# The order of the first three MLP blocks, the split of the first loads, the warming and a late sum in a two-layer decoder trunk

## The chip, the cores and the metric

One core of a Trainium2 chip runs the whole program. The metric is the device time of one execution in microseconds (us). The engines are TensorE (PE, matmuls), VectorE (DVE), ScalarE (ACT), GpSimd (POOL) and SyncE (SP, which issues DMAs); ACT and POOL issue DMAs too.

## The reference

The program computes two layers of a decoder trunk in float32, with 512 tokens of width 1024. Layer 0 has a latent attention mixer (MLA), layer 1 a gated linear attention mixer (GLA). Behind each mixer stands an MLP with a squared ReLU and 4096 hidden columns, and at the end a norm:

```python
def sq_relu_mlp(xn, w_up, w_down):
    hid = jnp.square(jax.nn.relu(xn @ w_up))
    return hid @ w_down

for i in range(DEPTH):
    x = x + mixer_i(rms_norm(x, norm_mix[i]))
    x = x + sq_relu_mlp(rms_norm(x, norm_mlp[i]), w_up[i], w_down[i])
return rms_norm(x, final_norm)
```

## The kernel before

**Numbers in two parts.** A float32 operand is split into a high and a low part that PE takes. ACT writes the high part of weights (`wh`, L112), DVE the low part (`wl`, L115). A product is three matmuls a tile: high by high, high weight by low data, low weight by high data. `wh` and `wl` have three buffers each.

**The start.** `load_x` (L168) loads x in eight parts of 256 KB, `load_part` (L1559) the first weights (`wraw_ckv`, 1 MB) in three, k-tiles 0 to 2, 2 to 4 and 4 to 8; ACT's queue takes x parts 0 and 2 and the gains (L1563), SP's the rest. `wraw` of the next product follows on SP. While they come, ten matmuls on ones (L1576, two records each in the profile) keep PE busy. For each weight part ACT and DVE split it (L112, L115), then scale and split the x parts with it (`scaled`, L245 on ACT and L246 on DVE, tiles `set`). The first phase of PE is 48 matmuls of 512 columns on the eight `set` pairs (L120 to L122); then the next product begins, whose weights are `wraw`, cut by `piece` in L451 and after.

**The MLP.** Up and down projections are each done in blocks by a scheme of seven products in place of eight. A product is 24 matmuls of 256 columns (L825): 16 with `wh` and 8 with `wl` (the latter in pairs on one weight tile). Eight blocks b make the hidden columns. `up_block(b)` gives a list of steps: s1 makes product 11, s2 21, s5 T1, s6 T2, s3 22, s7 T3, s4 T4 (s0 prepares). Bank x1 of PSUM holds 11 and then 21; x5 holds T1 and then 22; the bank `seed` (there is one, `b2`) starts as a copy of 11 (L925 on ACT) and takes T2, T3 and T4 one after the other, adding to what it holds. Between them it is read: after T2 by ACT (L951, `u2`), after T3 by DVE (L963, `q`, with the copy `p5` of T1), after T4 by `finish` (L889 on DVE, then a square on ACT, L890). DVE also makes sums of weight quarters: L948 and L954 for T2 and 22. The tiles `mt` (four buffers) hold `p1`, `p5` and `u2`; weight quarters lie in `raw` (five buffers) and come over SP (L864) or, adding to what is there, over POOL (L878).

`down_block(s)` gives the steps of the down projection, which stand between those of later up blocks. At the end of an MLP, L1043 to L1045 add the last products to the residual; L1045, `acc[4] += acc[6]`, is the late sum.

**What sets the order.** The program is written as straight code. Each engine runs its instructions in the order in which a scheduler lays them out from the order of the code, and waits on semaphores. Around the change the list returned by `up_block` and the loop over blocks in the MLP decide. In the loop, all steps of block 0 come first, then all of block 1 and so on; a down step is put behind every second one.

## Time and profile before

| | us |
|---|---|
| three runs | 1067.56, 1068.91 (median), 1069.22 |
| the profiled execution | 1068.29 |
| its span | 1066.6 |
| PE busy | 1048.6 (98%) |
| DVE busy | 856.7 (80%) |
| ACT busy | 640.1 (60%) |

The profiled execution's own time is 1.7 above its span, which runs from the first to the last recorded instruction. All times within the trace count from the start of the span. A row of a timeline has the start, the length, the engine, the line, the operation with output and inputs, the shape, a count where equal neighbours are joined, and in brackets how long the engine had been idle and what ended that. Busy time of PE contains overlaps of pipelined matmuls, so their pace is read from starts.

### The profile page before, as it was taken

How to read it: one execution, taken by the hardware profiler on the slowest of the kernel's cores; microseconds unless marked ns; L12 is line 12 of the kernel's file. 1: busy time of each engine (PE TensorE's matmuls, PEld its weight loads, DVE VectorE, ACT ScalarE, POOL GpSimd, SP SyncE). 2: the span in 40 equal slices, each digit the busy share in tenths (PEclk: the TensorE clock that was granted, in tenths of full speed). 3: DMA queues.
4: the chain of work that ended last, by engine and by line, in shares of the span. 5: the costliest groups of instructions: out<-in, count | busy, mean ns of one | idle time of the engine just before them, and what ended most of it. 6: DMA issues, size and time to landing. Idle time of an engine off the chain costs nothing.

```text
span 1066.6 us, 17924 instructions
## 1 busy us (share of the span) xinstructions
PE 1048.6 (98%) x7322; PEld 967.8 (91%) x7322; DVE 856.7 (80%) x1185; ACT 640.1 (60%) x934; POOL 77.9 (7%) x104
## 2 busy tenths in 40 slices
PE   8999999999999999999999999999999999999997
PEld 6788888989999999998788888888999999999986
DVE  6789879899899789966565654668999799799865
ACT  6577645665666776654334734655666667775734
POOL 6400000000000000030000000001000000000000
PEclk9999999999999999999999999999999999999999
DMA  6412016865554663351122212238564555653412
GB/s 204 105 50 79 1 40 196 180 179 137 166 139 132 178 147 117 94 193 43 50 80 80 80 48 71 80 98 216 163 137 139 169 129 158 187 128 103 139 39 80
DMA packets 113874, 126.76 MB, mean 119 GB/s; under 512 B 8592, under 2 KB 85664, under 8 KB 113792
## 3 DMA queue, kind: packets, MB, share of 16 engines
q1 hardware_dynamic: 98048, 107.62, 31.7%
q0 software_dynamic: 13792, 16.80, 10.1%
q10 hardware_dynamic: 1952, 1.21, 0.4%
q8 instruction: 57, 0.93, 0.4%
q14 instruction: 25, 0.20, 0.1%
HBM read 123.51 MB, written 2.10 MB: 118 GB/s over the span
## 4 chain that ended last, share of the span: by engine, by line
PE 93%; DVE 5%; DMA 1%; issue 1%; ACT 0%; SPq 0%; DVEq 0%
PE ps L825 46%; PE ps L120 13%; PE ps L122 13%; PE ps L121 13%; PE ps L137 2%; DVE wl L115 2%; PE ps L1406 2%; DMA wraw_ckv<-in_mla_w_in_dram 1%; PE ps L1445 0%; PE ps L684 0%; DVE raw L948 0%; PE ps L685 0%; PE ps L683 0%; PE ps L682 0%; PE ps L681 0%
## 5 line engine op out<-in xcount | busy, mean ns | idle before, releaser
L112 ACT ACTIVATE wh<-raw 128x1024 fp32r<-128x1024 f32 x208 | 219.7, 1059 | 139.6 <-PE ps L825 86.1
L115 DVE TENSOR_TENSOR wl<-raw,wh 128x1024 fp32r<-128x1024 f32 x208 | 251.5, 1220 | 22.6 <-ACT wh L112 22.0
L825 PE MATMUL ps<-h,wh 128*128 128x256 f32 x1344 | 166.6, 276 | 0.0
L825 PEld LDWEIGHTS ps<-h,wh 128*128 128x128 f32 x1344 | 159.2, 188 | 0.0
L120 PE MATMUL ps<-set,wh 128*128 128x512 f32 x232 | 91.6, 395 | 1.7 <-ACT set L245 1.7
L121 PE MATMUL ps<-set,wh 128*128 128x512 f32 x232 | 91.5, 394 | 1.0 <-DVE set L246 0.9
L825 PE MATMUL ps<-h,wl 128*128 128x256 f32 x672 | 90.4, 277 | 1.8 <-DVE wl L115 1.8
L122 PE MATMUL ps<-set,wl 128*128 128x512 f32 x232 | 91.3, 394 | 0.0
L112 ACT ACTIVATE wh<-wraw 128x1024 fp32r<-128x1024 f32 x41 | 43.0, 1057 | 73.7 <-PE ps L122 41.5
L825 PEld LDWEIGHTS ps<-h,wl 128*128 128x128 f32 x672 | 82.7, 188 | 2.2 <-DVE wl L115 2.2
L878 POOL DMA_DIRECT2D raw<-in_mlp_w_up_dram x20 | 25.8, 1290 | 701.2 <-DVE raw L931 309.0
L890 ACT ACTIVATE q<-q 128x512 f32<-128x512 f32 x64 | 40.3, 630 | 52.9 <-DVE q L889 52.6
L115 DVE TENSOR_TENSOR h<-q,h 128x1024 fp32r<-128x1024 f32 x44 | 53.7, 1222 | 8.3 <-ACT h L112 8.3
L120 PE MATMUL ps<-wh,set 128*128 128x512 f32 x144 | 59.6, 414 | 0.0
L115 DVE TENSOR_TENSOR wl<-wraw,wh 128x1024 fp32r<-128x1024 f32 x41 | 50.3, 1229 | 10.6 <-ACT wh L112 10.5
L122 PE MATMUL ps<-wh,set 128*128 128x512 f32 x144 | 56.3, 391 | 0.0
L121 PE MATMUL ps<-wl,set 128*128 128x512 f32 x144 | 56.2, 390 | 0.0
L121 PEld LDWEIGHTS ps<-set,wh 128*128 128x128 f32 x232 | 44.1, 190 | 11.0 <-DVE set L246 1.9
L120 PEld LDWEIGHTS ps<-set,wh 128*128 128x128 f32 x232 | 43.8, 189 | 10.9 <-ACT set L245 1.9
L122 PEld LDWEIGHTS ps<-set,wl 128*128 128x128 f32 x232 | 44.0, 190 | 9.1
L112 ACT ACTIVATE h<-q 128x1024 fp32r<-128x1024 f32 x44 | 46.0, 1049 | 0.8 <-DVE q L1024 0.8
L825 PE MATMUL ps<-T0h,wh 128*128 128x256 f32 x128 | 32.7, 280 | 5.0 <-DVE q L963 5.0
(512 smaller groups left out, 2779.0 us busy)
## 6 DMA issues: line engine op xcount, KB each, us to landing
raw<-in_mlp_w_down_dram SPq DMA_DIRECT2D x38, 1024.0 KB, 5.2
raw<-in_mlp_w_up_dram SPq DMA_DIRECT2D x68, 512.0 KB, 5.7
wraw<-in_gla_w_in_dram SPq DMA_DIRECT2D x11, 1024.0 KB, 5.2
raw<-in_mlp_w_up_dram POOLq DMA_DIRECT2D x20, 512.0 KB, 6.4
raw<-in_mlp_w_down_dram POOLq DMA_DIRECT2D x6, 1024.0 KB, 9.0
wraw<-in_mla_w_o_dram SPq DMA_DIRECT2D x8, 512.0 KB, 4.9
wraw<-in_gla_w_o_dram SPq DMA_DIRECT2D x8, 512.0 KB, 4.7
xT<-in_x_dram SPq DMA_DIRECT2D x6, 256.0 KB, 7.9
```

Of the source, the lines that this page charges most:

```text
L112: raised.append(order(ACT.activation(hi, src, AF.Copy)))
L115: return lo_eng.tensor_tensor(lo, src, f(hi), ALU.subtract)
L120: PE.matmul(psum, wh, xh, start=start, stop=False, **kw)
L121: PE.matmul(psum, wh, xl, start=False, stop=False, **kw)
L122: PE.matmul(psum, wl, xh, start=False, stop=stop, **kw)
L137: PE.transpose(psum, src, ident[: src.shape[0], : src.shape[0]])
L825: return PE.matmul(p[:, m * TH : (m + 1) * TH], w[i][:, k - k0, m * P : (m + 1) * P], x[k][j], start=start, stop=stop, skip_group_check=True,)
L878: POOL.dma_start(t, rows(half, trail), accum_op=ALU.add)
L890: ACT.activation(qs, qs, AF.Square)
L1406: PE.matmul(p[:, t * 64 : (t + 1) * 64].rearrange("p (n c) -> p n c", c=m), k[:, sl], later, start=True, stop=True)
```

## The change

**The start.** The first weights come in four parts of two k-tiles. ACT's queue issues the gains first, then x parts 0, 2, 3 and 4; SP's the weight parts and x parts 1, 5, 6 and 7. The warming has 15 matmuls. The split of the second product's weights is put behind the last `set` by `issue_after`.

**The blocks.** `up_block` returns other lists for blocks 0 to 2, block 2 also keeps a copy `p1` of its first product, and the read of bank `x5` (`third`) and the doubled sum (`twice`) move with them. The loop takes the steps of blocks 0, 1 and 2 in turn by a row of numbers. The products then follow as T1, T2, 22, T3 of block 0, T1 of block 1, T4 of block 0, 22 and T2 of block 1, 11 of block 2, T3 of block 1, 21 of block 2, T4 of block 1, T1 of block 2. Between any two on one `seed` bank, from T3 of block 0 to the end of block 1, another product stands.

**The late sum** leaves the callback and comes after the last third product.

```diff
--- before.py
+++ after.py
@@ -243,7 +243,7 @@
             hi, lo = slot(self.tag), slot(self.tag)
             g = gcol(self.g, self.g0 + j)
             self.copies[j] = order(ACT.activation(hi, src, AF.Copy, scale=g))
-            DVE.scalar_tensor_tensor(lo, src, g, f(hi), ALU.mult, ALU.subtract)
+            self.low = DVE.scalar_tensor_tensor(lo, src, g, f(hi), ALU.mult, ALU.subtract)
             self.out[j] = (hi, lo)
 
         def add(self, j, src):
@@ -451,7 +451,8 @@
 
         raw = col_chunk(w_in, 0, 256)
         for j in range(2):
-            w = piece(raw[:, :, j * P : (j + 1) * P], ND, P)
+            with tc.issue_after(nrm.copies[-1].ins), tc.issue_after(nrm.low.ins):
+                w = piece(raw[:, :, j * P : (j + 1) * P], ND, P)
             p = bank("c")
             a_type(p, w, X)
             if j == 0:
@@ -914,7 +915,7 @@
                 v["a21"], v["a22"] = unit(1, 0), unit(1, 1)
                 v["x1"] = bank("u")
                 product(v["x1"], a, "11", True)
-                if b == 1:
+                if b in (1, 2):
                     v["p1"] = mt()
                     ACT.activation(v["p1"], v["x1"], AF.Copy)
                 else:
@@ -942,17 +943,29 @@
                 product(v["x1"], v["a12"], "21", False)
                 finish(pairs(v["x1"]), 0, first)
 
+            def twice():
+                DVE.tensor_tensor(v["s"], v["s"], v["a11"], ALU.add)
+
             def s6():
-                if b == 1:
+                if b in (1, 2):
                     seed(v["p1"])
-                DVE.tensor_tensor(v["s"], v["s"], v["a11"], ALU.add)
+                if b != 1:
+                    twice()
                 product(v["b2"], v["s"], "T2", False)
                 v["u2"] = mt()
                 ACT.activation(v["u2"], v["b2"], AF.Copy)
+                if b == 1:
+                    third()
 
             def s3():
+                if b == 1:
+                    twice()
                 DVE.tensor_tensor(v["a12"], v["a12"], v["s"], ALU.add)
                 product(v["x5"], v["a12"], "22", False)
+                if b != 1:
+                    third()
+
+            def third():
                 c = q[1][:, 0:2]
                 DVE.tensor_tensor(c, pairs(v["x5"]), pairs(v["u2"]), ALU.add)
                 finish(c, 0, second)
@@ -967,7 +980,9 @@
                 product(v["b2"], v["a22"], "T4", False)
                 finish(pairs(v["b2"]), 1, first)
 
-            return [s0, s1, s2, s5, s6, s3, s7, s4] if b < 2 else [s1, s5, s2, s6, s3, s7, s4]
+            if b == 1:
+                return [s0, s1, s2, s5, s3, s6, s7, s4]
+            return [s0, s1, s2, s5, s6, s3, s7, s4] if b == 0 else [s1, s2, s5, s6, s3, s7, s4] if b == 2 else [s1, s5, s2, s6, s3, s7, s4]
 
         def down_block(s):
             last = s == NB // 2 - 2
@@ -1042,7 +1057,6 @@
                 def u3(p4):
                     DVE.tensor_tensor(acc[5], p4, acc[5], ALU.add)
                     DVE.tensor_tensor(acc[6], p4, acc[6], ALU.add)
-                    DVE.tensor_tensor(acc[4], acc[4], acc[6], ALU.add)
 
                 product(7, v["21"], b12, u3 if last else None)
 
@@ -1053,6 +1067,8 @@
             def p3():
                 DVE.tensor_tensor(v["S"], v["12"], v["S"], ALU.add)
                 product(3, v["S"], b22)
+                if last:
+                    DVE.tensor_tensor(acc[4], acc[4], acc[6], ALU.add)
 
             def p4():
                 a = quarter(1, 1)
@@ -1163,10 +1179,14 @@
         for b in range(2):
             blocks[b].pop(0)()
         downs = []
-        for b in range(NB):
-            for i, step in enumerate(blocks[b]):
+        for b in (0, 0, 0, 0, 1, 0, 1, 1, 2, 1, 2, 1):
+            blocks[b].pop(0)()
+        assert not blocks[0] and not blocks[1]
+        downs = down_block(0)
+        for b in range(2, NB):
+            for i, step in enumerate(blocks[b], 7 - len(blocks[b])):
                 step()
-                if downs and (i % 2 or (b % 2 and i == 6)):
+                if downs and (i in (2, 3, 5) if b == 2 else i % 2 or (b % 2 and i == 6)):
                     downs.pop(0)()
             if b % 2 and b < NB - 1:
                 downs += down_block(b // 2)
@@ -1558,24 +1578,27 @@
     def load_part(k0, k1):
         SP.dma_start(raw0[:, k0:k1], src0[:, k0:k1])
 
+    ACT.dma_start(gains, t_in["gains"])
+    load_part(0, 2)
     load_x(ACT, 0)
-    load_part(0, 2)
-    ACT.dma_start(gains, t_in["gains"])
     load_x(SP, 1)
     load_x(ACT, 2)
     load_part(2, 4)
-    load_x(SP, 3)
-    load_part(4, 8)
-    for j in range(4, ND):
-        load_x(SP, j)
+    load_x(ACT, 3)
+    load_part(4, 6)
+    load_x(ACT, 4)
+    load_x(SP, 5)
+    load_part(6, 8)
+    load_x(SP, 6)
+    load_x(SP, 7)
     POOL.dma_start(pos_i, t_in["positions"])
     POOL.dma_start(invf, t_in["inv_freq"].to_broadcast([P, 32]))
     exp_set()
     warm = bank("c")
-    for _ in range(10):
+    for _ in range(15):
         PE.matmul(warm[:, :P], ones128, ones128, start=True, stop=True)
     w0 = []
-    for k0, k1 in ((0, 2), (2, 4), (4, 8)):
+    for k0, k1 in ((0, 2), (2, 4), (4, 6), (6, 8)):
         w = piece(raw0[:, k0:k1], k1 - k0, KL, tc.keep_in_program_order)
         w0 += [(w, i) for i in range(k1 - k0)]
         for j in range(k0, k1):
```

PE where T3 of block 0 ends and what follows it, before. `ps_2289` is the `seed` bank of block 0, `T0h` to `T3h` are parts of the data, `wl_2495` the low weights of T3 and `wh_2525` the high weights of T4.

```order
1060 L825 MATMUL ps_2289<-T0h_1953,wl_2495 128x256 x2
1061 L825 MATMUL ps_2289<-T1h_2041,wl_2495 128x256 x2
1062 L825 MATMUL ps_2289<-T2h_2129,wl_2495 128x256 x2
1063 L825 MATMUL ps_2289<-T3h_2332,wl_2495 128x256 x2
1064 L825 MATMUL ps_2289<-T0h_1953,wh_2525 128x256
1065 L825 MATMUL ps_2289<-T0l_1954,wh_2525 128x256
```

The same place after the change, where the bank is `ps_2299` and `ps_2535` is bank `x5` of block 1.

```order
1060 L826 MATMUL ps_2299<-T0h_1963,wl_2505 128x256 x2
1061 L826 MATMUL ps_2299<-T1h_2051,wl_2505 128x256 x2
1062 L826 MATMUL ps_2299<-T2h_2139,wl_2505 128x256 x2
1063 L826 MATMUL ps_2299<-T3h_2342,wl_2505 128x256 x2
1064 L826 MATMUL ps_2535<-T0h_1963,wh_2536 128x256
1065 L826 MATMUL ps_2535<-T0l_1964,wh_2536 128x256
```

T4 of block 0, which came right behind T3, has moved 20 rows on; T1 of block 1 stands there.

DVE around the read of that bank after T3, before the change (L963; L957 is the read of bank `x5`).

```order
389 L957 TENSOR_TENSOR q_2263<-ps_2400,mt_2460 128x512
390 L115 TENSOR_TENSOR wl_2557<-raw_2251,wh_2556 128x1024
391 L889 SCALAR_TENSOR_TENSOR q_2263<-q_2263,rstd_2337 128x512
392 L948 TENSOR_TENSOR raw_2251<-raw_2251,raw_2157 128x1024
393 L963 TENSOR_TENSOR q_2263<-ps_2289,mt_2429 128x512
394 L954 TENSOR_TENSOR raw_2159<-raw_2159,raw_2251 128x1024
395 L889 SCALAR_TENSOR_TENSOR q_2263<-q_2263,rstd_2337 128x512
396 L115 TENSOR_TENSOR wl_2590<-raw_2251,wh_2589 128x1024
397 L889 SCALAR_TENSOR_TENSOR q_2262<-ps_2289,rstd_2337 128x512
```

And after it, where L976 is the read after T3, L970 that of `x5`, L947 and L963 the two sums, and L890 `finish`.

```order
390 L947 TENSOR_TENSOR raw_2261<-raw_2261,raw_2167 128x1024
391 L963 TENSOR_TENSOR raw_2169<-raw_2169,raw_2261 128x1024
392 L970 TENSOR_TENSOR q_2273<-ps_2410,mt_2470 128x512
393 L115 TENSOR_TENSOR wl_2567<-raw_2259,wh_2566 128x1024
394 L890 SCALAR_TENSOR_TENSOR q_2273<-q_2273,rstd_2347 128x512
395 L976 TENSOR_TENSOR q_2273<-ps_2299,mt_2439 128x512
396 L115 TENSOR_TENSOR wl_2599<-raw_2169,wh_2598 128x1024
397 L890 SCALAR_TENSOR_TENSOR q_2273<-q_2273,rstd_2347 128x512
398 L115 TENSOR_TENSOR wl_2629<-raw_2261,wh_2628 128x1024
399 L890 SCALAR_TENSOR_TENSOR q_2272<-ps_2299,rstd_2347 128x512
```

The two sums have moved from around the read to the place ahead of L970; behind the read comes a split (`wl_2599`) at once, and the finish of T4 (the last row) has one more split ahead of it.

DVE at the end of the first MLP, before: L1045 is the late sum, `wl_5163` the low weights that PE's next product takes.

```order
577 L1043 TENSOR_TENSOR xT<-ps_5033,xT 128x4x256
578 L1044 TENSOR_TENSOR sum_0_2244<-ps_5033,sum_0_2244 128x1024
579 L889 SCALAR_TENSOR_TENSOR q_4954<-ps_4962,rstd_2337 128x512
580 L1045 TENSOR_TENSOR xT<-xT,sum_0_2244 128x4x256
581 L115 TENSOR_TENSOR wl_5163<-raw_5155,wh_5162 128x1024
582 L115 TENSOR_TENSOR wl_5191<-raw_5155,wh_5190 128x1024
583 L115 TENSOR_TENSOR wl_5221<-raw_4994,wh_5220 128x1024
584 L115 TENSOR_TENSOR h_5283<-q_4042,h_5283 128x1024
```

And after: the late sum is L1071.

```order
578 L1058 TENSOR_TENSOR xT<-ps_5047,xT 128x4x256
579 L1059 TENSOR_TENSOR sum_0_2254<-ps_5047,sum_0_2254 128x1024
580 L890 SCALAR_TENSOR_TENSOR q_4968<-ps_4976,rstd_2347 128x512
581 L115 TENSOR_TENSOR wl_5176<-raw_5168,wh_5175 128x1024
582 L115 TENSOR_TENSOR wl_5204<-raw_5168,wh_5203 128x1024
583 L115 TENSOR_TENSOR wl_5234<-raw_5008,wh_5233 128x1024
584 L115 TENSOR_TENSOR h_5296<-q_4056,h_5296 128x1024
585 L1071 TENSOR_TENSOR xT<-xT,sum_0_2254 128x4x256
```

The late sum has moved behind three weight splits and a split of `h`.

## Prediction

> **What bounds the kernel now.** I read the page first: its span, its table of engines, and then who TensorE (PE) waits for.
>
> ```profile
> span 1066.6 us, 17924 instructions
> ...
> PE 1048.6 (98%) x7322; PEld 967.8 (91%) x7322; DVE 856.7 (80%) x1185; ACT 640.1 (60%) x934; POOL 77.9 (7%) x104
> ```
> ```profile
> PE ps L825 <- DVE q L963: 5.0, 4, 1.5
> PE ps L825 <- DVE wl L115: 1.8, 2, 1.0
> PE ps L120 <- ACT set L245: 1.7, 1, 1.7
> PE ps L121 <- DVE set L246: 0.9, 1, 0.9
> ```
>
> PE is busy for 1048.6 of 1066.6 us, and the change takes no matmul out of a product. It can only gain where PE idles. The list (total us, times, longest) names 5.0 us in four waits on L963, 1.8 in two waits on a weight split, and 2.6 in two waits at the start. Those three places are the three parts of the change. Next the timeline of PE around the first of the four waits, and at the second (start, duration, instruction, idle time before it).
>
> ```profile
> 214.23 0.40 PE L825 MATMUL ps<-T0h,wl 128*128 128x256 f32 x2
> ...
> 214.94 0.40 PE L825 MATMUL ps<-T3h,wl 128*128 128x256 f32 x2
> 216.84 0.39 PE L825 MATMUL ps<-T0h,wh 128*128 128x256 f32 x1 [1.50 <-DVE q L963]
> ...
> 218.78 0.39 PE L825 MATMUL ps<-T0h,wl 128*128 128x256 f32 x2
> ...
> 219.46 0.39 PE L825 MATMUL ps<-T3h,wl 128*128 128x256 f32 x2
> 231.73 0.39 PE L825 MATMUL ps<-T0h,wh 128*128 128x256 f32 x1 [1.00 <-DVE q L963]
> ```
>
> Two things are to be seen. A wait costs more than its idle figure: two matmuls start from 214.94, so without a wait the next would start at about 215.18; it starts at 216.84, 1.66 late, and a first matmul of 0.39 for 0.28 adds 0.11. The idle 1.50 so stands for 1.77 lost, some 0.27 more. And the pace differs on both sides: six matmuls take 214.94 - 214.23 = 0.71 us before the wait (118 ns each), and 219.46 - 218.78 = 0.68 after it (113 ns). PE has a slow and a quick pace here, and the wait seems to switch it.
>
> **Part 1, the blocks.** The bank that T2, T3 and T4 share must be read by L963 before T4 may add to it. DVE and ACT around that read, and around the next one:
>
> ```profile
> 214.96 1.22 DVE L948 TENSOR_TENSOR raw<-raw,raw 128x1024 f32<-128x1024 f32 x1
> 216.10 0.68 DVE L963 TENSOR_TENSOR q<-ps,mt 128x512 f32<-128x512 f32 x1
> ...
> 219.89 0.69 DVE L889 SCALAR_TENSOR_TENSOR q<-ps,rstd 128x512 f32<-128x512 f32 x1 [0.24 <-PE ps L825]
> ```
> ```profile
> 221.15 0.58 ACT L925 ACTIVATE ps<-mt 128x512 f32<-128x512 f32 x1
> ```
>
> T3 ends at about 215.2 and L963 is read out at 216.78. The change puts a whole product (T1 of block 1) between T3 and T4. A product is 24 matmuls, 24 x 0.1133 = 2.72 us at the quick pace. T4 then starts at about 218.0, and the read has 1.2 us to spare if DVE reaches it when it does today. DVE does: two adds (L948 and L954, 1.22 each) move ahead of the evacuation of block 0's second half, into an idle stretch, and after that a split and a finish stand before the read, as today. So all four waits should go: 5.0 + 4 x 0.27 = 6.1 us gross.
>
> What is late next? Block 1's T2 needs the bank again, seeded from a copy of its first product. Today T4 ends near 219.7, DVE's finish runs 219.89 to 220.58, ACT squares, and the seed ends at 221.73: 2.0 us after T4's end. In the new order one product of 2.72 us lies between (22 of block 1), so 0.7 us is spare. That is the tightest place; a split of 1.22 us ahead of the finish on DVE would use it up. Block 1's own T3 and T4 have a product between them as well, with the same spare 1.2 us, and a third block shares the scheme. Nothing is added on PE; two copies to SBUF replace seeds of the same form (0.58). The order also loads one weight quarter of block 2 a second time, which holds up two later loads; their first use is far enough off that I take it as nothing, and at most the delay of one 512 KB load, some 1.3 us at the rate shown below, if that cover is gone.
>
> Against that stands the pace. If a wait switches PE from 118 to 113 ns, then without it the slow pace goes on. For how long, the trace shows at one kind of place only:
>
> ```profile
> 240.01 2.03 PE L825 MATMUL ps<-h,wh 128*128 128x256 f32 x16
> ...
> 439.11 1.98 PE L825 MATMUL ps<-h,wh 128*128 128x256 f32 x16
> ```
>
> The first down product takes 2.03 for 16 matmuls where a later one takes 1.98: it turns PE slow, (2.03 - 0.28)/15 = 117 ns against 113, and yet the later ones are quick again with no wait listed between 231.73 and the end of the MLP. So the slow pace can end by itself, and I take it that it does so after that down product. Up to it, nine products run in the new order from the old wait on (T1 of block 1, T4 of block 0, 22 and T2 of block 1, 11 of block 2, T3 of block 1, 21 of block 2, T4 of block 1, T1 of block 2): 9 x 24 x 0.0050 = 1.1 us per layer, about 2.0 for two layers with what the restart of today's quick pace costs taken off. Bounds: nothing, if the pace recovers at once; 3.1, half the gross gain, if it lasts somewhat longer. Part 1: -6.1 + 2.0 = -4.1 (-3.0 to -6.1).
>
> **Part 2, the late sum.** The end of the first MLP, DVE and then PE, and PE's same place in the second:
>
> ```profile
> 439.65 1.22 DVE L1045 TENSOR_TENSOR xT<-xT,sum 128x1024 f32<-128x1024 f32 x1
> 440.79 3.49 DVE L115 TENSOR_TENSOR wl<-raw,wh 128x1024 fp32r<-128x1024 f32 x3
> ```
> ```profile
> 442.06 1.19 PE L825 MATMUL ps<-h,wl 128*128 128x256 f32 x8 [0.97 <-DVE wl L115]
> ...
> 989.21 1.20 PE L825 MATMUL ps<-h,wl 128*128 128x256 f32 x8 [0.80 <-DVE wl L115]
> ```
>
> The sum of 1.22 stands right before the split that PE waits for. Moved behind three splits and one split of `h`, it lets the first split start at 439.65 and end at about 440.87; PE wants it after 16 matmuls from 439.11, at 439.11 + 16 x 0.1133 = 440.92. The wait goes, all but 0 to 0.1. Gain: 0.97 + 0.80 + 2 x 0.27 = 2.3, less 0.1: -2.2 (-2.0 to -2.3). The sum now precedes the fourth split; that one is behind work for three products, and is covered by them.
>
> **Part 3, the start.** PE, then ACT, then DVE; then windows of PE (length, busy time, matmul records, granted clock, DMA share, GB/s), and of the DMA engines (length, clock, DMA share, GB/s), with the issue of `gains` (KB, us to landing).
>
> ```profile
> 6.74 0.73 PE L120 MATMUL ps<-set,wh 128*128 128x512 f32 x2 [1.73 <-ACT set L245]
> ...
> 14.20 0.39 PE L120 MATMUL ps<-set,wh 128*128 128x512 f32 x1
> 15.52 0.50 PE L121 MATMUL ps<-set,wh 128*128 128x512 f32 x1 [0.94 <-DVE set L246]
> ...
> 20.87 0.39 PE L120 MATMUL ps<-set,wh 128*128 128x512 f32 x1
> ```
> ```profile
> 2.31 1.28 ACT L127 ACT_TABLE_LOAD   x1 [2.31 <-issue]
> 5.03 0.63 ACT L112 ACTIVATE wh<-wraw_ckv 128x512 fp32r<-128x512 f32 x1 [1.44 <-DMA wraw_ckv<-in_mla_w_in_dram]
> ...
> 12.24 1.06 ACT L112 ACTIVATE wh<-wraw_ckv 128x1024 fp32r<-128x1024 f32 x1 [1.84 <-DMA wraw_ckv<-in_mla_w_in_dram]
> ...
> 17.91 1.06 ACT L112 ACTIVATE wh<-wraw 128x1024 fp32r<-128x1024 f32 x1 [1.63 <-DMA wraw<-in_mla_w_in_dram]
> ```
> ```profile
> 14.53 3.03 DVE L246 SCALAR_TENSOR_TENSOR set<-xT,gains,set 128x512 fp32r<-128x512 f32 x4
> 19.00 2.62 DVE L115 TENSOR_TENSOR wl<-wraw,wh 128x1024 fp32r<-128x1024 f32 x2 [1.44 <-ACT wh L112]
> ```
> ```profile
> 7.40:10.80 3.40, 3.35 (x9) 0.50 0.95 255
> 10.80:14.20 3.40, 3.40 (x17) 0.99 1.07 384
> ```
> ```profile
> 2.50:6.50 4.00, 1.00 0.98 330
> 9.50:12.20 2.70, 0.75 1.06 394
> gains<-in_gains_dram ACTq DMA_DIRECT2D x1, 25.5 KB, 4.6
> ```
>
> The first phase is 48 matmuls of 512 columns; it ends at 20.87, when the next weights' product begins. PE stands after 14.20 because the (4,8) part of the weights is one transfer: ACT waits for it until 12.24, splits all of it, and DVE then works through four sets in a row, 14.53 to 17.56. In halves, sets 4 and 5 need not wait for the last quarter, and PE no longer idles there. But the same bytes come through the same engines by the same time, so the last x part and the last set hardly move; I let the phase end near 19.7. The next product has its first `wl` at 19.00 + 1.31 = 20.31 and needs it after two matmuls of 0.227, so it can't start before 19.85 unless its weights land sooner. Gain: 20.87 - 19.85 = 1.0.
>
> The clock: from 7.40 to 10.80 PE ran at 0.50 and did 9 matmuls, then 17 in the same time. Five more warming matmuls (two records each) shorten the gap of 1.73 ahead of the first product, so this stretch may be granted full clock: worth 8 x 0.2 = 1.6 by itself (3.40/17 is 0.2). It is hidden, since loads set the end of the phase. The page "TensorE: Matmul & The Clock Gate" (Trainium skill, Part 1) says that what is issued in the first 3.4 us or so of activity runs at half clock and what follows at full; here a half-clock window came after a full one, behind a gap. Read by that page alone, longer warming would bring those 1.6 us, and the sum would be 0.6 lower.
>
> Bounds: two queues moved 330 GB/s (2.50 to 6.50), one 394 (9.50 to 12.20). 512 KB more on two queues takes 0.26 us longer at the lower rate, so the second weights land up to that much later. ACT now issues an x part that waits for the landing of `gains`, and its table load (1.28) and first split (5.03 today) stand behind that. `gains` goes out first, at about 0.8, and lands by 0.8 + 4.6 = 5.4; with the issue and the table load the first split would be at 7.0 at the latest, 2.0 later than today, and I expect half a microsecond to one. The first product would be at 8.7 at the latest, and 48 x 0.227 = 10.9 us later, at 19.6, the phase would still be done in time at full clock. So 0.3 is left at the least that I take for likely, with the rest among the rivals. At most 1.6, if the next weights land 0.6 sooner: that is what the stretch from 2.50 to 6.50 would save at the rate of 394. Part 3: -1.0 (-0.3 to -1.6). "DMA: Bandwidth & Descriptors" (Trainium skill, Issuing engines are not separate DMA queues) says that transfers issued by different engines run on the same 16 DMA engines; the two rates agree that a second queue adds no bandwidth, and by that rule alone part 3 would be worth nothing.
>
> **Sum.** -4.1 - 2.2 - 1.0 = -7.3. The profiled execution took 1068.29 us (span 1066.6), so 1061.0 for it; it lies 0.62 below the median of 1068.91, which gives 1061.6.
>
> **Rivals.**
> - *The slow pace stays (slower).* With both waits of an MLP gone nothing switches PE back. From 217 to the end of the MLP at about 440 are 223 us, at 4.2% slow (0.71 against 0.68): 9.4 per layer, 18.7 in all, against a gross gain of 6.1 + 2.3 + 1.0 = 9.4: about 1078. It decides from where the slow pace lasts half of that, 110 us; there the time is the old one, 1068.9. For it: the pace before the wait was steady, and changed only at the wait. Against it: the row at 240.01, slow, is followed by quick products with no wait. Full 0.07, about half way 0.07.
> - *The pace costs nothing.* It recovers within a product or starts quick. Then part 1 is -6.1: 1059.6. Nothing in the rows tells how it begins. 0.16.
> - *The seed is late.* Its 0.7 us are used up by a split of 1.22 that DVE does first; T2 of block 1 waits 0.5 + 0.27, in each layer: +1.5, 1063.1. On DVE one split now stands ahead of that finish; it can run while T4 does, if its `wh` is there and its buffer free, and costs the spare time if not. 0.14.
> - *The start gives nothing*, as the rule on queues has it, or loses, if ACT starts 2.0 late and the half-clock window stays (19.6 + 1.6 = 21.2, 0.3 late): 1062.6 to 1062.9. For it: both rates. 0.10. *The start goes by the clock*, as the rule on the clock has it: 1.6, 1061.0. Against it: the second weights land at 17.8 whatever PE does. 0.04.
>
> **Chances and range.** My forecast has 0.42, and with the neighbours that leave it faster (0.16, 0.14, 0.10, 0.04) 0.86; of these a twentieth may sum to less than is measurable. What a measurement can tell is 0.2%, 2.1 us, so faster means below 1066.8. Faster 0.83, same 0.08, slower 0.09. The low end takes all the best bounds: 1068.9 - 6.1 - 2.3 - 1.6 = 1058.9, rounded down to 1058.5. The high end goes by part 1 at -3.0, the start at nothing and a late seed of 1.5, 1068.9 - 3.0 - 2.0 + 1.5 = 1065.4, a little up towards the half-way pace: 1066.0. Left out are the two cases of the slow pace, 0.14, and tails.
>
> **What would show it.** In the profile after: no wait on the evacuation of T3 in the list of PE's waits; no wait on the first split at the end of the MLPs; 24 matmuls in about 2.83 us between 216 and 240 and 2.72 beyond. The start is right if PE enters the second phase between 19.3 and 20.3, with no idle time near 14. A pace of 118 ns after 250 would make me wrong, as would a new wait on the seed at about 223, or first products later than 7.5 with the second phase at 20.8 or later.

## The result and the profile after

The changed kernel takes 1066.07 us (median of 15 runs, 1065.48 to 1066.90) where the kernel before took 1068.67 beside it (15 runs, 1067.34 to 1070.45). The ratio is 0.9978, with a 95% interval of 0.9971 to 0.9985: some 2.3 to 2.6 us less, a gain that is real and a third of the 7.3 that were forecast. The forecast of 1061.6 was missed by 4.5, and its range, to 1066.0, by less than 0.1.

The list of PE's waits in the changed kernel (total us, times, longest) is this:

```profile
span 1063.8 us, 17962 instructions
...
PE 1055.4 (99%) x7332; PEld 975.8 (92%) x7332; DVE 856.6 (81%) x1186; ACT 642.4 (60%) x937; POOL 78.8 (7%) x104
```
```profile
PE ps L1599 <- DVE ones L175: 1.2, 1, 1.2
PE ps L685 <- ACT set L665: 0.3, 1, 0.3
```

Every wait that the change aimed at is gone: the four on the read after T3, the two of the late sum, the two at the start. Yet PE's busy time rose from 1048.6 to 1055.4 us for the same products. The time that PE no longer waits, it spends computing more slowly. To see where, take the mean's matmul of each norm as a mark, in the timelines of both kernels, the kernel before first.

```profile
197.36 1.02 PE L255 MATMUL ps<-acc,inv 128*128 128x512 f32 x2
...
1046.57 0.59 PE L1654 MATMUL ps<-acc,inv 128*128 128x256 f32 x2
```
```profile
195.24 1.02 PE L255 MATMUL ps<-acc,inv 128*128 128x512 f32 x2
195.69 0.68 PE L826 MATMUL ps<-x4h,wh 128*128 128x256 f32 x1
...
1044.03 0.59 PE L1677 MATMUL ps<-acc,inv 128*128 128x256 f32 x2
```

The first mark comes 2.12 us sooner, which is the start's gain; the last 2.54 sooner. So the two MLPs together, whose waits cost 8.4 us before, gained only 0.4. Counting matmul records in fixed windows shows why. The columns are the window, its length, PE's busy time and the records in it, the granted clock, and the DMA share and rate; the kernel before, then the changed one.

```profile
250.00:310.00 60.00, 60.00 (x531) 1.00 0.54 158
340.00:380.00 40.00, 40.00 (x356) 1.00 0.49 145
800.00:860.00 60.00, 60.00 (x532) 1.00 0.54 159
```
```profile
250.00:310.00 60.00, 60.00 (x512) 1.00 0.55 159
340.00:380.00 40.00, 40.00 (x356) 1.00 0.51 148
800.00:860.00 60.00, 60.00 (x512) 1.00 0.52 150
```

531 in 60 us is 113 ns each and 512 some 118 ns, since a window also counts the matmuls that its edges cut; PE is busy all the time at a granted clock of 1.00 in both. The DMA queues move as much in both (158 and 159 GB/s from 250 to 310), so transfers do not explain it. The changed kernel is slow at 250 and quick again at 340. Product by product, the slow pace holds from the mean (195.7) to the second pair of down products:

```profile
325.12 0.40 PE L826 MATMUL ps<-T0h,wl 128*128 128x256 f32 x2
...
325.83 0.40 PE L826 MATMUL ps<-T3h,wl 128*128 128x256 f32 x2
326.06 2.03 PE L826 MATMUL ps<-h,wh 128*128 128x256 f32 x16
```

Six matmuls in 0.71 us, 118 ns, right up to 326; from 331.7 on they take 113. In the second MLP the quick pace returns at 878.7. A pace of 118 ns after 250 is the sign that the prediction had named for being wrong.

Three places answer to the steps of the forecast. T3 ends near 213.1, DVE has read its bank at 214.86, and T4 begins at 215.88; the seed for T2 of block 1 ends at 220.75, and that product begins at 221.53. Nothing waits.

```profile
214.18 0.68 DVE L976 TENSOR_TENSOR q<-ps,mt 128x512 f32<-128x512 f32 x1
...
218.91 0.69 DVE L890 SCALAR_TENSOR_TENSOR q<-ps,rstd 128x512 f32<-128x512 f32 x1 [1.17 <-PE ps L826]
```
```profile
220.17 0.58 ACT L926 ACTIVATE ps<-mt 128x512 f32<-128x512 f32 x1
```

At the start, the first product comes at 6.81, the second phase at 18.38 in place of 20.87, and the weights that bound it are split from 16.56 on (17.91 before). From 7.40 to 10.80 the clock is at 1.00, where it was at 0.50 before.

```profile
6.81 0.73 PE L120 MATMUL ps<-set,wh 128*128 128x512 f32 x2
...
18.38 0.39 PE L120 MATMUL ps<-set,wh 128*128 128x512 f32 x1
```
```profile
16.56 1.06 ACT L112 ACTIVATE wh<-wraw 128x1024 fp32r<-128x1024 f32 x1 [2.09 <-DMA wraw<-in_mla_w_in_dram]
```
```profile
7.40:10.80 3.40, 3.34 (x15) 1.00 0.80 285
```

### The profile page after: what moved, and what is told of

The parts are those of the page before. It is cut to its first block, busy times and chain, and to the rows that moved or that the text cites. A ratio compares the mean times of both kernels' runs of the same rounds, so it can differ in the third digit from the quotient of the medians.

```text
span 1063.8 us, 17962 instructions
## 1 busy us (share of the span) xinstructions
PE 1055.4 (99%) x7332; PEld 975.8 (92%) x7332; DVE 856.6 (81%) x1186; ACT 642.4 (60%) x937; POOL 78.8 (7%) x104
## 3 DMA queue, kind: packets, MB, share of 16 engines
q10 hardware_dynamic: 2240, 1.73, 0.5%
## 4 chain that ended last, share of the span: by engine, by line
PE 96%; DVE 2%; ACT 0%; DMA 0%; issue 0%; ACTq 0%; DVEq 0%
PE ps L826 51%; PE ps L120 13%; PE ps L122 13%; PE ps L121 13%; PE ps L1426 2%; PE ps L137 1%; PE ps L1465 0%; PE ps L1432 0%; PE ps L1412 0%; PE ps L685 0%; PE ps L686 0%; PE ps L684 0%; PE ps L682 0%; PE ps L683 0%; DVE stat L695 0%; DMA gains<-in_gains_dram 0%
## 5 line engine op out<-in xcount | busy, mean ns | idle before, releaser
L121 PE MATMUL ps<-hl,wh 128*128 128x512 f32 x96 | 37.4, 389 | 0.0
```

The costliest lines, as they stand in the source:

```text
L121: PE.matmul(psum, wh, xl, start=False, stop=False, **kw)
```

## The experiments

Two theories stood at first. **The pace**: every part gains what it takes away in waits, and the loss lies in a slow pace of PE that nothing interrupts now. **The rival**: the new order, or the earlier phase of the loads, brings costs of its own. The runs of one batch share their runs of the kernel before; its medians were 1069.56, 1068.22, 1068.23, 1068.11 and 1068.35 us.

### The parts apart

`e1_start` is the kernel before with the three start edits (loads, 15 warming matmuls, `issue_after`). `e2_late` moves only the late sum:

```diff
                 def u3(p4):
                     DVE.tensor_tensor(acc[5], p4, acc[5], ALU.add)
                     DVE.tensor_tensor(acc[6], p4, acc[6], ALU.add)
-                    DVE.tensor_tensor(acc[4], acc[4], acc[6], ALU.add)
...
                 product(3, v["S"], b22)
+                if last:
+                    DVE.tensor_tensor(acc[4], acc[4], acc[6], ALU.add)
```

`e3_blocks` has only the edits of `up_block` and of the loop over blocks.

> The kernel before with the start alone changed (first loads, warming, the split put behind the last set). The pace theory (each part gains what it was meant to, and the loss lies in PE's slow pace alone) takes the 2.1 us that the mean of the first MLP comes earlier in the changed kernel, and all of it stays: 2.1 less than before, the pace as before. The forecast of 1.0 for this part would be 1.0 less. A theory that the start gives its gain back later, by a changed phase of loads, expects no difference.

> The kernel before with the late sum alone moved. Both theories expect the two waits at the end of the MLPs to be gone, 2.2 us less than before (2.0 to 2.3), and no change of pace.

> The kernel before with the order of the first three blocks alone changed. Pace theory: the four waits go (6.1 us less), and 39 products in each MLP, from the old wait to about 109 us later, run at 2.83 in place of 2.72 us: 39 x 0.108 = 4.2, some 0.2 less for two that are slow in both, so 8.0 more for two MLPs. Together 1.9 us more than before. The forecast for this part was 4.1 less. A theory that the new order brings work of its own in PE's way would show waits or gaps between products, not a steady 118 ns.

Measured: `e1_start` 1067.07 (ratio 0.9991, 0.9974 to 1.0008), `e2_late` 1066.75 (0.9981, 0.9966 to 0.9996), `e3_blocks` 1071.05 (1.0013, 0.9997 to 1.0028). The late sum alone is a gain, and the forecast (0.2%) lies inside its wide interval (0.04 to 0.34%). The blocks alone are no gain: the interval reaches from no change to 0.28% slower, where 4.1 us less (0.9962) had been forecast, and the list of waits of `e3_blocks` holds none on the read after T3. Its windows are those of the changed kernel:

```profile
250.00:310.00 60.00, 60.00 (x511) 1.00 0.57 166
340.00:380.00 40.00, 40.00 (x356) 1.00 0.50 145
800.00:860.00 60.00, 60.00 (x511) 1.00 0.57 164
```

So the loss came with the blocks, as pace, not as gaps. The start alone is inconclusive by time: its trace has the first mark 2.1 us sooner, but its span is only 1.5 shorter, and two of the waits that stayed acted otherwise than in the kernel before. One, on the read after T3 in the second MLP (762.60, 1.50 us idle), left the pace slow, where the same wait, as long, ends it in the kernel before. The other, at the end of the first MLP, began it:

```profile
437.01 1.98 PE L826 MATMUL ps<-h,wh 128*128 128x256 f32 x16
439.56 1.21 PE L826 MATMUL ps<-h,wl 128*128 128x256 f32 x8 [0.57 <-DVE wl L115]
440.61 2.05 PE L826 MATMUL ps<-h,wh 128*128 128x256 f32 x16
```

The 16 matmuls ahead of the wait take 1.98, those behind it 2.05. A wait does not simply repair the pace; it may also spoil it.

### Waits put in on purpose

If waits switch the pace, a short one behind the mean should pay. In `e4_wait` the changed kernel got this; `e7_wait3` and `e8_wait6` do the ACT line three and six times:

```diff
         kept(nrm.mean())
+        x4 = quad["21"][0][0][:, :1]
+        kept(ACT.activation(x4, nrm.ms[:, :1], AF.Identity, bias=f(x4), scale=0.0))
```

> The changed kernel with one short wait of PE put behind the mean's matmul of each MLP: ACT adds 0 x mean to a column of the data part that PE's next product reads, which leaves the data as they are. Pace theory: a wait of PE, of any cause, ends the slow pace. All products from 196 on then run at 113 ns; 45 products of each MLP gain 0.108 each, 4.9 us, and each wait costs about 0.6 to 0.9: 8.0 us less than the changed kernel (7 to 8.6), near 1058. Rival, that the slow pace hangs on what the products read and write (where operands lie) and not on a wait: the pace stays at 118 and the two waits cost 1.2 to 1.8 more than the changed kernel.

> As the run with one wait behind the mean, but ACT writes the column three times in a row, so PE waits longer. In that run a wait of 0.35 us in the first MLP left the pace at 118 ns and one of 0.8 in the second ended it. Theory that the length decides: both waits are now 0.8 or more, both MLPs run at 113 ns from there, and the first MLP is 4.9 us shorter than with the short wait less 0.4 for the longer one; 1058.4 for the whole (1057.5 to 1059.5). Rival, that it is where the restart falls against some other cycle, or the second MLP's addresses, and not the length: the first MLP stays at 118, or the second falls back to 118, and the run is at 1063 or more.

> As before with six writes of the column: waits of about 1.4 us. If the length decides, 113 ns in both MLPs, and 0.6 us more per MLP than with three: about 1059.6. If it is chance, either MLP may be at 118, 4.5 us more for each.

Measured: `e4_wait` 1062.84 (0.9952, 0.9935 to 0.9970), `e7_wait3` 1059.94 (0.9926, 0.9911 to 0.9941), `e8_wait6` 1064.42 (0.9964, 0.9953 to 0.9976). In `e4_wait` the wait of the first MLP left the pace slow and that of the second ended it. The rows of the timeline, then the windows:

```profile
196.90 0.39 PE L826 MATMUL ps<-x4h,wh 128*128 128x256 f32 x1 [0.35 <-ACT x4h L1174]
...
745.00 0.38 PE L826 MATMUL ps<-x4h,wh 128*128 128x256 f32 x1 [0.77 <-ACT x4h L1174]
```
```profile
250.00:310.00 60.00, 60.00 (x511) 1.00 0.57 163
...
800.00:860.00 60.00, 60.00 (x532) 1.00 0.53 154
```

`e7_wait3` has both MLPs quick, the first from a wait of 0.94 us on, the second from one of 1.36:

```profile
197.94 0.39 PE L826 MATMUL ps<-x4h,wh 128*128 128x256 f32 x1 [0.94 <-ACT x4h L1175]
```
```profile
250.00:310.00 60.00, 60.00 (x532) 1.00 0.58 166
...
800.00:860.00 60.00, 60.00 (x532) 1.00 0.56 152
```

With no product changed, waiting 2.3 us more in all makes the kernel 6.1 us faster than the changed one (1059.94 against 1066.07, both with the kernel before within 0.5 us of each other). That shows the pace as the place of the loss. But the length of the wait does not decide, as I had thought after `e4_wait`: in `e8_wait6` the longest wait of all, 2.24 us, left the second MLP at 118 ns.

```profile
198.43 0.39 PE L826 MATMUL ps<-x4h,wh 128*128 128x256 f32 x1 [1.82 <-ACT x4h L1175]
...
746.44 0.39 PE L826 MATMUL ps<-x4h,wh 128*128 128x256 f32 x1 [2.24 <-ACT x4h L1175]
```
```profile
198.40:201.80 3.40, 3.37 (x16) 0.55 0.77 123
...
800.00:860.00 60.00, 60.00 (x512) 1.00 0.57 163
```

(There, too, the wait of 1.82 us was followed by 3.4 us at a granted clock of 0.55; the one of 2.24 was not.) The wait of 1.82 left the first MLP at 118 ns as well, up to the down products at 244.

This trace is of the slowest of the eight executions of `e8_wait6`, 1068.94 us; the other seven took 1063.15 to 1065.57. The difference of some 4.5 us is what the expectation gives for one MLP at 118 ns, so the same waits probably left one MLP more quick in the others; no trace shows it. A wait can set the pace either way, and its length does not tell which.

### Where the operands lie

The product right ahead of the mean has its weights in a tile `w` that shares its place with the data tile T3; it runs at 120 ns in the kernel before and in the changed one. In the compiled program, `w` and the data x that it meets begin at 96 bytes past a multiple of 256, the other weights (`wh`, `wl`) at 160. That gave the third theory: the distance sets the pace. `e9_w64` moves `w` by 64 bytes in a tile made 128 bytes wider; `e11_before_w64` does so in the kernel before; `e12_w64_h` also puts the data of the first down product of a pair of blocks, 32 bytes off, where the others are, 64 off. `e13_wh96` moves all `wh` and `wl` by 64 bytes.

```diff
-                    w = v["11"] = tuple(up.tile([P, KH, 256], F32R, tag=f"T{KH - 1}{x}", name=uname("w")) for x in "hl")
+                    w = v["11"] = tuple(
+                        up.tile([P, KH * 256 + 32], F32R, tag=f"T{KH - 1}{x}", name=uname("w"))[:, 16 : 16 + KH * 256].rearrange("p (k n) -> p k n", k=KH)
+                        for x in "hl"
+                    )
```
```diff
-                    c = 0 if turn[1] != s else 40
+                    c = 40
```
```diff
+    sb.tile([P, 16], F32, tag="pad", name=uname("pad"))
     inv_d = inv_tile(D, const)
```

> The changed kernel with the weights of the product ahead of the mean (tile w, which shares its place with data tile T3) moved by 64 bytes inside a wider tile; the order of all engines is the same. In the program as built, w and the data x that meet it both begin at 96 bytes past a multiple of 128; all other up weights (wh, wl) begin at 32, 64 bytes off the data. Theory that the place sets the pace: the product with w runs at 113 in place of 120 ns, no slow pace begins there, and the MLPs run at 113 without any wait: 0.16 and some 45 x 0.108 = 4.9 for each MLP, 10.1 us less than the changed kernel, about 1056. Rival, that the pace behind the mean is drawn anew by the float32 matmul or by chance: 118 ns behind it in one MLP or both, 4.9 us more for each.

> As the last, and the data h of the first down product of each pair of blocks, which begins at 64 (32 bytes off the weights), is put where the other products have theirs (64 bytes off). Place theory: these products run at 113 in place of 117 ns: two halves of 24 matmuls, 0.08 each, in three places of each MLP, 1.0 us less in all, about 1055. If these products are what brings a slow pace back to the quick one, and a slow pace still begins somewhere, it lasts longer here than with them.

> The kernel before with the weights w moved by 64 bytes. Place theory: the 8 products from w to the first wait run at 113 ns, 0.16 + 7 x 0.108 = 0.9 less for each MLP, 1.8 in all; the waits of L963 and of the late sum stay and may draw a slow pace anew, 118 ns for a while, as one did in the run with the start alone.

> The changed kernel with 64 bytes put ahead of the weight buffers, so wh and wl begin at 96 as the data x and T do; the down data h move with them and stay 64 bytes off. Place theory: all up products run at 120 ns, down products at 113 or 118 as now. 24 up products that are at 2.83 go to 2.88 and some 32 at 2.72 go to 2.88 in each MLP: 24 x 0.05 + 32 x 0.16 = 6.3, about 12.6 in all, near 1079; the mixers may change as well. Rival, that place does not matter: the pace as now.

Measured: `e9_w64` 1058.83 (0.9909, 0.9896 to 0.9922), `e12_w64_h` 1066.95 (0.9993, 0.9971 to 1.0015), `e11_before_w64` 1068.53 (1.0003, 0.9995 to 1.0012), `e13_wh96` 1076.58 (1.0075, 1.0057 to 1.0092). The timeline of `e9_w64` on `w`:

```profile
194.39 0.39 PE L830 MATMUL ps<-x0h,w 128*128 128x256 f32 x2
...
195.07 0.39 PE L830 MATMUL ps<-x3h,w 128*128 128x256 f32 x2
```

Six matmuls in 0.68 us: the product with `w` runs at 113 ns now. That the distance matters is shown twice, by this and by `e13_wh96`, where the up products slowed down to between 118 and 120 (its windows are slow in all three places, 517, 345 and 518 records). But the slow pace behind the mean was still there in `e9_w64`; this half of the theory failed. It ended earlier, at 244, in the first MLP and at 749 in the second, and so the time is the best of all that ran. Its windows, then those of `e12_w64_h`:

```profile
217.60:230.00 12.40, 12.40 (x108) 1.00 0.44 147
250.00:310.00 60.00, 60.00 (x532) 1.00 0.55 159
```
```profile
250.00:310.00 60.00, 60.00 (x512) 1.00 0.57 164
340.00:380.00 40.00, 40.00 (x342) 1.00 0.50 145
800.00:860.00 60.00, 60.00 (x531) 1.00 0.60 170
```

`e12_w64_h` shows one thing that ends the slow pace where nothing waits. With the down products that lie 32 bytes off taken away, the first MLP stays at 118 ns to its end, at 340 too; with them, at 117 ns each, it turns quick behind one of them: behind the first pair in `e9_w64` (244), behind the second in the changed kernel (331.7). They are slower themselves, and pay for it.

It is not the only one. In the second MLP of the three kernels with `w` moved (`e9_w64`, `e11_before_w64`, `e12_w64_h`) the pace turned quick three products behind the mean, at 748.7, 753.9 and 757.2, at a step of 143 ns between two starts in place of 118, which the list of waits does not hold. In `e9_w64`:

```profile
748.75 0.30 PE L830 MATMUL ps<-T0h,wh 128*128 128x256 f32 x1
748.89 0.28 PE L830 MATMUL ps<-T0l,wh 128*128 128x256 f32 x1
```

So the 7.2 us between `e9_w64` and the changed kernel are only in a small part the product with `w` itself (2 x 0.16); the rest goes with 29 and 41 fewer products at 118 ns (70 x 0.108 = 7.6), and why the slow pace ended sooner in the first MLP is not shown. Two of the twelve executions of `e12_w64_h` took 1075.74 and 1076.09 us, the others 1065.91 to 1067.65: a second MLP that stays slow to its end would cost as much (93 x 0.108 = 10.0), but no trace shows these two.

In `e11_before_w64` most of the forecast gain did not come: in the first MLP the seven products behind the mean stayed at 118 ns, and the wait that ends at 231.5 left 118 ns up to the down products at 240.

### What begins the slow pace

The mean's matmul is the other thing that stands there: float32, 0.86 us in two records. `e6_mean_r` does it in one pass in the split format. `e14_w64_mean_r` does this and moves `w`, and `e15_w64_mean_r2` repeats that with the data in their old place; `e16_up128` makes the shift of the data alone that `e14_w64_mean_r` had (there x3, x7 and the low part of T3 had stayed).

```diff
-                DVE.tensor_tensor(self.acc, self.acc, s, ALU.add)
+                if hasattr(self, "quad") and self.seen == self.n - 1:
+                    self.sums = tmp(dt=F32R)
+                    DVE.tensor_tensor(self.sums, self.acc, s, ALU.add)
+                else:
+                    DVE.tensor_tensor(self.acc, self.acc, s, ALU.add)
...
+            if hasattr(self, "quad"):
+                return PE.matmul(self.ms, inv_r, self.sums, start=True, stop=True)
```
```diff
-    PADS = dict(stage=224, up=320, masks=256, keep=128, decayed=320, down_w=64)
+    PADS = dict(stage=224, up=448, masks=256, keep=128, decayed=320, down_w=64)
```

> The changed kernel with the mean's matmul of the MLP norms in the split format, in one pass of about 0.23 us, in place of float32, which takes 0.86: the sums of squares are rounded when the last one is written. It asks what begins the slow pace. If the float32 matmul does: the 16 matmuls right behind the mean run at 113 ns, and the MLPs with them; with 0.6 less for each mean about 1055. If it is the product ahead of it, whose weights lie in another tile and which runs at 120 ns in every trace: the pace behind the mean is 118 as before, and only the 0.6 for each mean are gained (1064.8). Some vector work is laid out in another order here, so a wait near 197 may come in addition.

> The changed kernel with both things changed that stood ahead of the slow pace: the weights w moved by 64 bytes, and the mean of the MLP norms in the split format in one pass (sums of squares rounded when the last one is written); the few instructions around the mean are held in about the old order. Each alone left 118 ns behind the mean. Theory that both a product at 120 ns and the float32 matmul begin the slow pace: now 113 ns right behind the mean and through both MLPs; 0.6 for the mean, 0.16 for w, 45 x 0.108 = 4.9 in each MLP, less a possible short wait on one split: 10.8 less than the changed kernel, near 1055.3 (1054.5 to 1056.5). Rival, that the pace falls either way by chance or by something else that stands there: 118 ns behind the mean, 1060 or more.

> The last experiment again, without a shift that it had beside its two changes: there all data of the up products began 128 bytes lower (224 past a multiple of 256 in place of 96). Here they lie where the changed kernel has them; w is moved by 64 bytes and the mean runs in one pass in the split format. Theory that a product at 120 ns and the float32 matmul are each able to begin the slow pace, and that the last run was slow by its shift: 113 ns from the mean on, or from the wait of about 1.5 us on one split that the last run showed near 204, and 4 to 5 us less in each MLP than the changed kernel: 1056 to 1059. Rival, that something else behind the mean begins it: 118 ns behind it up to a wait or to a product that lies 32 bytes off; 1061 to 1067.

> The changed kernel with nothing but a pad of 320 bytes made 448, which puts all data of the up products 128 bytes lower; the order is the same. Theory that the distance counts modulo 256, and not 128, and that the last run was slow by it: up products at 118 ns throughout both MLPs, also behind products that lie 32 bytes off, some 54 products slower by 0.108 in all: 5 to 7 in each MLP less the 4 that are slow now, about 1070 to 1076. Rival, that the distance modulo 128 is all: the pace as in the changed kernel, 1066.

Measured: `e6_mean_r` 1070.64 (1.0017, 1.0006 to 1.0028), with new waits on splits of up to 1.9 us that DVE's changed order brought; `e14_w64_mean_r` 1075.59 (1.0067, 1.0052 to 1.0081), 20 us above its expectation; `e15_w64_mean_r2` 1060.86 (0.9929, 0.9916 to 0.9941); `e16_up128` 1075.85 (1.0071, 1.0055 to 1.0087). The timeline of `e6_mean_r` around the mean:

```profile
195.91 0.39 PE L262 MATMUL ps<-tmp,inv_r 128*128 128x512 f32 x1
...
198.02 0.40 PE L834 MATMUL ps<-x4h,wl 128*128 128x256 f32 x2
...
198.73 0.40 PE L834 MATMUL ps<-x7h,wl 128*128 128x256 f32 x2
```

Still 118 ns behind a mean of one short pass. In `e15_w64_mean_r2`, with `w` at 113 as well, too. There it turned quick at 204.3 and 748.4, at a start 0.19 us late (as `e6_mean_r` did at 201.0), ahead of the wait of 1.21 us on a split that follows in each MLP; the first of the two places:

```profile
204.00 0.28 PE L838 MATMUL ps<-T3l,wh 128*128 128x256 f32 x1
204.31 0.50 PE L838 MATMUL ps<-T0h,wl 128*128 128x256 f32 x2
```

Neither the float32 format nor the 120 ns of `w` is needed. That the mean's matmul comes between two streams of 256 columns is what all these kernels have left in common; no run takes it away, and what in it begins the slow pace stays open.

`e16_up128` was meant to explain the slow `e14_w64_mean_r`, and does: 128 bytes more of padding, not one instruction changed or moved, and both MLPs run at 118 ns from end to end, 9.8 us above the changed kernel. Its windows:

```profile
250.00:310.00 60.00, 60.00 (x512) 1.00 0.56 160
340.00:380.00 40.00, 40.00 (x342) 1.00 0.51 145
800.00:860.00 60.00, 60.00 (x512) 1.00 0.59 170
```

The data of the up products then lie 64 bytes past the weights, modulo 256, where they lay 64 bytes short of them. Short of them, both paces occur and last; past them, the up products with `wh` and `wl` in the two kernels that had it came to 118 ns within 16 matmuls, in `e14_w64_mean_r` behind quick down products too. (In `e9_w64` eight matmuls with the low weights of `w` and those with the low part of T3 lie that way as well and ran at 113, so this holds for streams and not for every matmul.)

## Why the prediction was wrong, point by point

- **The waits on T3's read (6.1 us gross): right.** All four are gone. The read has 1.0 us to spare where 1.2 was forecast (214.86 to 215.88), the seed 0.8 where 0.7 was (220.75 to 221.53).
- **The step that failed** is in part 1: "So the slow pace can end by itself, and I take it that it does so after that down product. Up to it, nine products run in the new order from the old wait on". The price was 2.0 us with a bound of 3.1. In the run the slow pace passed that down product (240.01 in the kernel before) and held to the next pair: from T3's end at 213 to 326 are 40 products, 38 without two that are slow in both kernels, 38 x 0.108 = 4.1 in each MLP. The marks say the same: 8.4 us of waits gone, 0.4 gained, 8.0 lost to the pace in both MLPs. With 6.1 gained and 8.0 lost the blocks were a loss of 1.9, where a gain of 4.1 had been forecast; `e3_blocks`, with its interval about no change and above, and `e7_wait3`, which gets 6 us back by waiting, bear that out. The row at 240.01 was read wrongly: it showed that such a product leaves a quick pace quick, and says nothing of whether it ends a slow one.
- **The rival "the slow pace stays"** had the mechanism, the price (9.4 per MLP for all of it) and even the case: "about half way", 110 us from the old wait, is what happened (213 to 326, 113 us). It gave 1068.9; the start's extra 1.1 and a price of 8.0 in place of 9.4 bring that to 1066.4, near the 1066.07 that were measured. It had 0.07 of the chances. Against the forecast, the pace cost 6.0 more and the start gave 1.1 more back; that the time came so close to the range is owed to the second. The two cases of the slow pace together lay outside the range; the rows that spoke for it (steady at 118 until the very wait) were better than the one against it.
- **The late sum (2.2): right.** No wait is left there, and `e2_late` alone took 0.19% off, with an interval of 0.04 to 0.34%.
- **The start (1.0, bounds 0.3 to 1.6): too small.** 2.1 us came, and the second phase began at 18.38, ahead of the 19.3 to 20.3 that were to show the forecast right. The rival by which the start gives nothing did not come. ACT's first split was late as forecast (5.52 for 5.03) and cost nothing. The bound that I put on the second phase, the landing of its weights, moved by 1.3 us (split from 16.56, not 17.91). The forecast took the landing as fixed but for 0.6. Why it moved that far is not settled; the rate over the first microseconds was higher by less than that needs (261 GB/s for 255 from 1 to 7 us). The half-clock stretch went, as the rival on the clock had it: 15 records from 7.40 to 10.80 in place of 9.
- **The clock's page.** Read by "TensorE: Matmul & The Clock Gate" (Trainium skill, Part 1) alone, the longer warming would give the start the 1.6 that the prediction estimated; 2.1 came, with the loads changed as well, and no run here parts the two.

## What to carry to other kernels

A wait that goes is worth its idle time only if the work behind it keeps its pace: before counting it as gained, compare the start-to-start time of equal instructions on both sides of the wait, and if they differ, price the rest of the stage at the slower one. When busy time rises as idle time falls, with the same instructions, look for a changed pace and not for a new wait. Where weights and data lie against each other in SBUF, modulo 256 bytes, was worth more here than the reordering; 128 bytes of padding cost 9.8 us; 64 bytes on one small tile won 7.2 over the changed kernel, mostly because the slow pace ended sooner, and won nothing in the kernel before. Where a pace can fall either way, one trace is one of several outcomes: set its time beside those of the other executions.

## What the runs showed of the hardware

- Matmuls of 256 columns in the split format (high and low parts) start every 113, 117, 118 or 120 ns at a granted clock of 1.00, with PE never idle. 120 goes with weights and data at the same place modulo 128 bytes (118 to 120 in `e13_wh96`), 117 with 32 bytes between them (120 in some places of `e14_w64_mean_r`), 113 or 118 with 64; where the data lie past the weights by 64, modulo 256, streams came to 118.
- With data 64 short of the weights the pace persists. It outlived 46 products in the changed kernel, and all of the first MLP in `e12_w64_h`. It can change at a wait, in either direction (0.57 us: quick to slow; 0.35, 1.82, 2.24: slow stayed slow; 0.77, 0.94, 1.36: slow to quick; 1.50: quick in the kernel before, still slow in `e1_start`), at a start only 0.025 us late, and behind products at 117 ns.
- A wait of 1.82 us was followed by 3.4 us at a granted clock of 0.55 (16 matmuls where 30 would fit), as the gap of 1.73 at the start was in the kernel before. A wait of 2.24 us in the same trace was not: 28 matmuls in the 3.4 us behind it, at 1.00.
- The fastest of these runs is `e9_w64`: 1058.83 us, ratio 0.9909 (0.9896 to 0.9922) to the kernel before.
